# Cross-attention keys and values projected two heads at a time, gates of the linear attention in one piece, skip term by a full matrix of ones

## The chip, the cores and the metric

The kernel runs on one core of a Trainium2 chip. The metric is the device time of one execution in microseconds (us), as the median over repeated runs. Engines are named as in the profile: PE (matrix multiplication, TensorE), DVE (VectorE), ACT (ScalarE), POOL (GpSimd) and SP (the queue that issues nearly all DMAs here). Each engine executes its own instruction stream strictly in order.

## The reference, cut to what matters

A two-layer encoder on 512 tokens of width 1024 (fp32). Each layer adds three mixers (attention, a long convolution called Hyena, gated linear attention), a cross attention into a memory of 256 tokens, and an MLP. The change touches three places: the keys and values of the cross attention, the skip of the long convolution, and the decay gates of the linear attention.

```python
def memory_cross_attention(hn, mn, wq, wk, wv, wo, qn, kn):
    q = rmsnorm((hn @ wq).reshape(B, L, X_HEADS, X_HEAD_DIM), qn)
    k = rmsnorm((mn @ wk).reshape(B, M, X_HEADS, X_HEAD_DIM), kn)   # 4 heads of 256
    v = (mn @ wv).reshape(B, M, X_HEADS, X_HEAD_DIM)
def hyena_filter_spectra(...):
    f = f / (jnp.sum(jnp.abs(f), axis=0, keepdims=True) + EPS)
def long_conv(u, spec, skip):
    return irfft(rfft(u) * spec) + u * skip
def gla_mixer(q, k, v, og, lr, w_lr, b_lr, onorm):
    logit = einsum(lr, w_lr) + b_lr
    g = jax.nn.log_sigmoid(logit) / GLA_NORMALIZER
```

## The kernel before, in words

**Matmuls.** Every fp32 product is three matmuls (`mm3`, L247 to L249): both operands are split into a high and a low part, and high by high, high by low and low by high are added in PSUM. Activations stay in SBUF as such pairs (`xh`/`xl`, for the memory `mnh`/`mnl`). Weights come from HBM in chunks of 128x1024 fp32 (512 KB). For each chunk SP issues a DMA into one of two raw buffers (`wr`), ACT casts it to the high part (`wh`, L231), DVE subtracts to the low part (`wl`, L232), and PE reads both; `wh` and `wl` have three buffers each. `wchunk` (L260) does that for two chunks, which are 256 output columns. A raw buffer is free again when DVE has subtracted, so a late split delays the weights behind it as well.

**Order of the work.** The phases of a layer are generators, and `ORDER0` and `ORDER` say by hand in which order their steps are recorded: `kv` (keys and values of the memory, `cross_kv`), `mx` (`mix_norm`, which makes the normalised input of the layer), `gp` and `gh` (gated linear attention), `at` (attention), `fi` (the filters of the convolution), `ga` (merge gates), `hy`, `me`, `wo`. A scheduler turns this into one stream for each engine. Weight splits are recorded ahead of what stands around them; small matmuls are marked late.

**The pieces touched.** `cross_kv` (L1139) projects the 256 memory tokens head by head, first four heads of v, then four of k: two chunks per head, and 48 matmuls of 256 columns (`mm3` with `wh,mnh`, 2 token tiles x 8 row tiles x 3). ACT evicts v (L1177); for k, ACT squares and sums (L1192), DVE computes a reciprocal root by integer and Newton steps (`rsqrt`, L342, eleven small instructions) and scales (L1197), PE transposes (L1203). Heads of kv stand ahead of `mx` in both lists, so their matmuls are what PE does while DVE and ACT normalise the input: `finish_stat` (L336, a matmul that sums squares over partitions from `hsum`, L328), rsqrt, `tok_bcast` (L358, a matmul that spreads the result), then eight tiles `nrm` (L384) and their split `xh`/`xl` (L242, L243). The first user of the normalised input is the low-rank projection in `gla_proj` (L886).

`filters` (L613) makes the spectra in eight groups (2 layers x 2 orders x 2 halves). The four of layer 0 run inside layer 0's mixers, the four of layer 1 inside layer 0's MLP. At the end of a group (L700 to L720) a matmul with one column of ones sums |f| over partitions into one row of PSUM (L706), two more matmuls make the same sums as columns (L708), DVE adds EPS and multiplies by the skip on that one row of 256 numbers (L712), and a matmul of a row of ones by that row spreads it over 128 partitions into the group's PSUM bank (L718).

`gla_proj` (L868) ends with the gates of four heads. For each: a matmul (L922), Abs on ACT (L925), min on DVE (L927), Exp on ACT (L928), all 128x512; then Ln (L933), a subtraction on POOL (L940), and two cumulative scans on DVE (L941, L943) with POOL copies (L948, L949), then exponentials (L952 to L954) and products on DVE (L959, L960). Exp, Ln and the merge gates' Tanh (L1072) don't share one activation table, so ACT loads a table (ACT_TABLE_LOAD) at a switch.

## Time and profile before

| | before |
|---|---|
| median of 3 runs | 2301.21 us (2300.2 to 2303.95) |
| the profiled execution | 2299.69 us |
| its span, first to last instruction | 2297.8 us |
| PE busy | 2211.1 us, 96% |
| DVE busy | 1535.5 us, 67% |
| ACT busy | 1013.0 us, 44% |
| POOL busy | 418.1 us, 18% |
| mean granted clock of PE | 0.985 |

The profiled execution is 1.5 us below the median. A busy share is a mean over 2.3 ms: stretches in which PE does not pause stand beside short ones in which DVE is busy throughout and PE waits for it. The idle time of an engine is listed with the instruction that ended it.

### The profile page before, as it was taken

Reading aid. Unit: us, or ns where it says so; the run is one execution under the profiler, and the core shown is the slowest. Engines: PE = TensorE matmul, PEld = TensorE weight load, DVE = VectorE, ACT = ScalarE, POOL = GpSimd, SP = SyncE. Lnnn points to the kernel's source line nnn. Section 1 sums busy time; section 2 is a strip of 40 time slices with the busy share of each in tenths; the row PEclk is TensorE's granted clock in tenths of the full one; section 3 lists DMA queues with packets and bytes.
Section 4 is the critical chain, followed back from the end, with each engine's and each line's share of the span. In section 5 each row is a group of like instructions: output and inputs, shape, how many; then the busy total and the mean of one; then the engine's idle time right before and its main releaser. Section 6 shows DMA issues by size and latency. Waiting matters only on the chain.

```text
span 2297.8 us, 29857 instructions
## 1 busy us (share of the span) xinstructions
PE 2211.1 (96%) x11432; PEld 1857.2 (81%) x11432; DVE 1535.5 (67%) x2491; ACT 1013.0 (44%) x1635; POOL 418.1 (18%) x353
## 2 busy tenths in 40 slices
PE   6989999998899999999999989999989999999999
PEld 6877888887678878888887978888867788888887
DVE  7799856869665755766476786667886566444445
ACT  5667744323344544443336577443323444433231
POOL 1141101224220101111051130012253101000004
PEclk9999999999999999999999999999999999999999
DMA  6423123123143133332244321242222422323222
GB/s 224 146 97 106 65 74 123 56 93 101 60 149 113 63 122 103 122 122 101 92 143 143 105 79 41 74 128 65 83 101 74 141 89 74 101 92 101 94 94 97
DMA packets 78966, 232.58 MB, mean 101 GB/s; under 512 B 9054, under 2 KB 10086, under 8 KB 78824
## 3 DMA queue, kind: packets, MB, share of 16 engines
q1 hardware_dynamic: 75656, 224.91, 29.7%
q0 software_dynamic: 3168, 5.77, 0.9%
q8 instruction: 90, 1.47, 0.3%
q14 instruction: 52, 0.43, 0.1%
HBM read 213.87 MB, written 16.78 MB: 100 GB/s over the span
## 4 chain that ended last, share of the span: by engine, by line
PE 78%; DVE 13%; ACT 3%; DMA 2%; issue 2%; POOL 1%; SPq 0%; DVEq 0%; ACTq 0%; POOLq 0%
PE ps L249 24%; PE ps L247 24%; PE ps L248 24%; DVE wl L232 3%; PE ps L533 1%; ACT wh L231 1%; DVE ts L796 1%; PE ps L520 1%; PE ps L542 1%; PE ps L544 1%; DMA wr<-in_x_wv_dram 1%; PE ps L521 1%; DMA F<-F 1%; DVE u L797 1%; DVE ts L587 1%
## 5 line engine op out<-in xcount | busy, mean ns | idle before, releaser
L232 DVE TENSOR_TENSOR wl<-wr,wh 128x1024 fp32r<-128x1024 f32 x340 | 432.7, 1275 | 257.6 <-ACT wh L231 253.1
L231 ACT CAST wh<-wr 128x1024 fp32r<-128x1024 f32 x344 | 357.9, 1042 | 554.1 <-PE ps L248 459.8
L249 PE MATMUL ps<-xh,wl 128*128 128x512 f32 x1344 | 532.8, 397 | 17.2 <-DVE wl L232 17.2
L247 PE MATMUL ps<-xh,wh 128*128 128x512 f32 x1344 | 534.3, 398 | 2.3 <-ACT wh L231 2.0
L248 PE MATMUL ps<-xl,wh 128*128 128x512 f32 x1344 | 532.3, 396 | 0.0
L249 PEld LDWEIGHTS ps<-xh,wl 128*128 128x128 f32 x1344 | 255.4, 190 | 72.6 <-DVE wl L232 20.9
L247 PEld LDWEIGHTS ps<-xh,wh 128*128 128x128 f32 x1344 | 255.6, 190 | 55.7 <-ACT wh L231 3.3
L248 PEld LDWEIGHTS ps<-xl,wh 128*128 128x128 f32 x1344 | 255.6, 190 | 50.4
L249 PE MATMUL ps<-hdh,wl 128*128 128x512 f32 x512 | 199.9, 390 | 0.0
L247 PE MATMUL ps<-hdh,wh 128*128 128x512 f32 x512 | 199.7, 390 | 0.0
L248 PE MATMUL ps<-hdl,wh 128*128 128x512 f32 x512 | 199.2, 389 | 0.0
L1344 DVE TENSOR_TENSOR macc<-ps,macc 128x512 f32<-128x512 f32 x96 | 66.1, 689 | 86.0 <-PE ps L249 86.0
L249 PEld LDWEIGHTS ps<-hdh,wl 128*128 128x128 f32 x512 | 96.1, 188 | 22.1 <-issue 2.3
L248 PEld LDWEIGHTS ps<-hdl,wh 128*128 128x128 f32 x512 | 96.1, 188 | 19.9
L247 PEld LDWEIGHTS ps<-hdh,wh 128*128 128x128 f32 x512 | 96.1, 188 | 19.9 <-issue 0.3
L1346 POOL TENSOR_TENSOR macc<-macc,rb 128x512 f32<-128x512 f32 x16 | 23.6, 1472 | 398.4 <-DVE macc L1344 398.4
L248 PE MATMUL ps<-wl,xh 128*128 128x256 f32 x320 | 91.5, 286 | 0.8 <-DVE wl L232 0.8
L247 PE MATMUL ps<-wh,xh 128*128 128x256 f32 x320 | 91.4, 286 | 0.1
L249 PE MATMUL ps<-wh,xl 128*128 128x256 f32 x320 | 91.3, 285 | 0.0
L248 PE MATMUL ps<-wl,mnh 128*128 128x256 f32 x256 | 77.0, 301 | 13.9 <-DVE wl L232 13.8
L1328 DVE TENSOR_TENSOR rl<-rl 128x512 f32<-128x512 f32 x64 | 44.7, 699 | 65.9 <-ACT rl L1327 65.9
L247 PE MATMUL ps<-wh,mnh 128*128 128x256 f32 x256 | 76.2, 298 | 7.8 <-ACT wh L231 7.8
(404 smaller groups left out, 4570.8 us busy)
## 6 DMA issues: line engine op xcount, KB each, us to landing
wr<-in_mlp_w_dram SPq DMA_DIRECT2D x128, 512.0 KB, 3.5
wr<-in_w_in_dram SPq DMA_DIRECT2D x108, 512.0 KB, 3.6
wr<-in_x_wv_dram SPq DMA_DIRECT2D x16, 512.0 KB, 3.6
wr<-in_x_wk_dram SPq DMA_DIRECT2D x16, 512.0 KB, 4.0
F<-ff SPq DMA_DIRECT2D x32, 256.0 KB, 2.3
F<-F SPq DMA_DIRECT2D x32, 256.0 KB, 5.2
wr<-in_w_out_dram SPq DMA_DIRECT2D x16, 512.0 KB
wr<-in_x_wq_dram SPq DMA_DIRECT2D x16, 512.0 KB, 3.6
```

The costliest lines, as they stand in the source:

```text
L231: r = self.nc.scalar.copy(hi, src)
L232: (lo_eng or self.nc.vector).tensor_tensor(lo, src, hi, op=ALU.subtract)
L247: mm(out, lh, rh, start=start, stop=False, skip_group_check=True)
L248: mm(out, lh, rl, start=False, stop=False, skip_group_check=True)
L249: mm(out, ll, rh, start=False, stop=stop, skip_group_check=True)
L520: nc.tensor.matmul(s, QH[:, tk], K2, start=True, stop=False)
L521: nc.tensor.matmul(s, QL[:, tk], K2, start=False, stop=True)
L533: nc.tensor.transpose(pt[:, k, i * P:(i + 1) * P], Pn[i][:, (2 * kp + k) * P:(2 * kp + k + 1) * P], self.ident)
L542: nc.tensor.matmul(ov, vv, TH[:, k], start=(kt == 0), stop=False, skip_group_check=True)
L1328: nc.vector.tensor_tensor(r, r, r, op=ALU.mult)
L1344: nc.vector.tensor_tensor(acc[m], ps, acc[m], op=ALU.add)
L1346: nc.gpsimd.tensor_tensor(acc[m], acc[m], rb, op=ALU.mult)
```

## The change

Four edits, in the order of the title, and one in the buffers.

1. `cross_kv` projects two heads at once. The host lays `x_wk` and `x_wv` out so that one chunk of 512 KB holds 256 rows by 512 columns. `proj_mem` reads four chunks per pair of heads and issues 48 matmuls of 512 columns into two PSUM banks. Squares, roots and scales follow for two heads together (one rsqrt of four columns where there were two of two). `kv` has five steps where it had nine, and stands in the lists anew: all four heads of v are recorded before `mx`, no head of k.
2. The chunks of `x_wv` go through three raw buffers of their own (`wraw`), issued after the last weight DMA recorded; those of `x_wk` stay in the ring `wr`.
3. The skip is multiplied before the sum over partitions: `hy_skip` comes as 128x256 (128 KB, the row repeated by the host), DVE forms (acc + EPS/128) x skip, ACT and DVE split it, and two matmuls of 256 columns with a 128x128 matrix of ones add it into the group's bank. L706 and L718 go.
4. The gates of four heads lie in one tile `ab` of 128x4x512: four Abs, then one Exp and one Ln of 128x2048.

```diff
-kv kv kv lx kv kv kv mx fi gp gp kv gp fi at at at gp at fi at at at gp ga0 at gp fi kv at kv ga0 at
+kv kv lx kv mx fi gp gp kv gp fi at at at gp at fi at at at gp ga0 at gp fi kv at ga0 at at ga0 at
...
-kv kv kv kv kv kv mx gp gp gp kv at at at at ga0 kv gp at at at ga0 at at gp at ga0 at at at at gp
-at at ga0 at gp gp gp at gh gh gh kv gh gh ga2 gh gh dft hy0 ga2 gh at gh at ga2 gh hy0 gh hy0 hy0
+kv kv kv mx gp gp gp kv at at at at ga0 gp at at at ga0 at at gp at ga0 at at at at gp at at ga0 at
+gp gp gp at gh gh gh kv gh gh ga2 gh gh dft hy0 ga2 gh at gh at ga2 gh hy0 gh hy0 hy0 me0 hy1 gh hy0
...
+    def proj_mem(self, W, hp, X, own):
+        ps = [self.ps("mm") for _ in range(2)]
+        for g in range(4):
+            raw = self.t("wraw", (P, 1024), F32, "wraw") if own else self.wbuf("wr")
+            with self.after(self.last_w) if self.last_w is not None else nullcontext():
+                self.last_w = self.nc.sync.dma_start(raw, W[hp, g])
...
+            with self.tc.high_priority(offset=SPLIT_AHEAD):
+                self.split(raw, hi, lo)
+            for mt in range(2):
+                tk = slice(mt * P, (mt + 1) * P)
+                for k in range(2):
+                    kt = 2 * g + k
+                    self.mm3(ps[mt], X[kt][0][..., tk], X[kt][1][..., tk], hi[:, k], lo[:, k], kt == 0, kt == 7)
+        return ps
...
+                skip = self.skip
+                self.load(skip, I["hy_skip"][l, o, c])
...
+                sa = self.t("F", (P, 2, 256), F32, "skip")[:, 0]
+                nc.vector.scalar_tensor_tensor(sa, acc, EPS / P, skip, op0=ALU.add, op1=ALU.mult)
+                sb = self.t("F", (P, 2, 256), F32R, "skip2")
+                self.split(sa, sb[:, 0], sb[:, 1])
+                with self.late("fr"):
+                    for x in range(2):
+                        nc.tensor.matmul(T4[0][:, 0], self.ones_r, sb[:, x], start=False, stop=(x == 1),
+                                         skip_group_check=True)
...
-                    nc.tensor.matmul(ps[0:1, 0:256], self.ones[:, 0:1], acc, start=True, stop=True)
...
-                row = self.rowbuf
-                self.load(row, I["hy_skip"][l, o, c])
-                nc.vector.scalar_tensor_tensor(row, ps[0:1, 0:256], EPS, row, op0=ALU.add, op1=ALU.mult)
...
-                    nc.tensor.matmul(T4[0][:, 0], self.ones[0:1, :], row, start=False, stop=True,
...
+        xs = self.t("ab4", (P, 4, L), F32, "ab")
         for h in range(4):
...
-            nc.scalar.activation(c, ps, AF.Abs, bias=b)
+            nc.scalar.activation(xs[:, h], ps, AF.Abs, bias=b)
...
-            nc.scalar.activation(c, c, AF.Exp, scale=-1.0)
...
-        for c in xs:
-            nc.scalar.activation(c, c, AF.Ln, bias=self.ones[:, 0:1])
+        nc.scalar.activation(xs, xs, AF.Exp, scale=-1.0)
+        yield
+        nc.scalar.activation(xs, xs, AF.Ln, bias=self.ones[:, 0:1])
...
-        for h in range(4):
-            w = self.wchunk(I["x_wk"][l], h)
...
+        for hp in range(2):
+            ps = self.proj_mem(I["x_wk"][l], hp, X, False)
```

**PE, start of layer 1.** Before, the sums for the normalised input (L336, `hsum`) stand behind 120 matmuls of the values (`wh`/`wl` with `mnh`/`mnl`):

```order
L248 MATMUL ps_10430<-wl_74,mnh_10281 128x256
L249 MATMUL ps_10430<-wh_70,mnl_10282 128x256
L336 MATMUL ps_10625<-consts,hsum_10107 128x1
L247 MATMUL ps_10430<-wh_72,mnh_10248 128x256
L336 MATMUL ps_10625<-consts,hsum_10107 128x1 x3
```

Now the same sums (L360 of the changed kernel) stand behind 15:

```order
L251 MATMUL ps_10116<-wh_73,mnh_10069 128x512
L252 MATMUL ps_10116<-wl_74,mnh_10069 128x512
L253 MATMUL ps_10116<-wh_73,mnl_10070 128x512
L360 MATMUL ps_10264<-ones,hsum_9917 128x1 x4
L251 MATMUL ps_10116<-wh_73,mnh_10069 128x512
```

The broadcast (L358 before, L382 now) follows 18 matmuls later before and 15 later now, and the first user of the normalised input (L886, now L913) stands behind 240 matmuls of 256 columns before (four heads of v, one of k) and behind 96 of 512 columns now (four heads of v).

**DVE, gates of layer 1.** Before, two weight splits (`wl`) stand behind the first scan (L941) of the fourth head:

```order
L943 SCALAR_TENSOR_TENSOR ab_11598<-reset_12221,mn_11600 64x512
L941 SCALAR_TENSOR_TENSOR ab_11605<-reset_12221,mn_11607 64x512
L950 TENSOR_TENSOR ab_11598<-ab_11598,small 128x512
L943 SCALAR_TENSOR_TENSOR ab_11605<-reset_12221,mn_11607 64x512
L941 SCALAR_TENSOR_TENSOR ab_11612<-reset_12221,mn_11614 64x512
L232 TENSOR_TENSOR wl_74<-wr_69,wh_72 128x1024
L232 TENSOR_TENSOR wl_75<-wr_68,wh_70 128x1024
L959 SCALAR_TENSOR_TENSOR qk_1677_10774<-qk_1677_10774,mn_11593 128x512
```

Now two of them stand behind the first scan (L966) of the first head:

```order
L954 TENSOR_SCALAR mn_11186<-ps_11183,consts 128x512
L954 TENSOR_SCALAR mn_11191<-ps_11188,consts 128x512
L966 SCALAR_TENSOR_TENSOR ab_11172<-reset_11795,mn_11176 64x512
L236 TENSOR_TENSOR wl_76<-wr_70,wh_71 128x1024
L236 TENSOR_TENSOR wl_74<-wr_69,wh_72 128x1024
L968 SCALAR_TENSOR_TENSOR ab_11172<-reset_11795,mn_11176 64x512
L966 SCALAR_TENSOR_TENSOR ab_11172<-reset_11795,mn_11181 64x512
```

The next `wl` comes eleven instructions after the last row shown, behind four more scans.

**ACT, gates of layer 1.** Before, between the last two heads' Abs (L925), Exp (L928) and Ln (L933) stand three table loads, and a fourth before L952:

```order
L925 ACTIVATE ab_11612<-ps_11610,consts 128x512
L933 ACT_TABLE_LOAD
L933 ACTIVATE ab_11605<-ab_11605,consts 128x512
L928 ACT_TABLE_LOAD
L928 ACTIVATE ab_11612<-ab_11612 128x512
L1072 ACTIVATE gt_11785<-ps_11760 128x512
L933 ACT_TABLE_LOAD
L933 ACTIVATE ab_11612<-ab_11612,consts 128x512
L231 CAST wh_72<-wr_69 128x1024
L952 ACT_TABLE_LOAD
```

Now one Exp (L956) and one Ln (L958) of 128x2048, with a merge gate's Tanh (L1097, `gt`) between them and two weight casts (L235) behind:

```order
L952 ACTIVATE ab_11172<-ps_11188,consts 128x512
L956 ACTIVATE ab_11172<-ab_11172 128x2048
L1097 ACTIVATE gt_11362<-ps_11337 128x512
L958 ACT_TABLE_LOAD
L958 ACTIVATE ab_11172<-ab_11172,ones 128x2048
L235 CAST wh_71<-wr_70 128x1024
L235 CAST wh_72<-wr_69 128x1024
L1097 ACT_TABLE_LOAD
```

In the whole program ACT has 17 table loads before and 9 now, and PE 11114 rows before and 10732 now.

## Rows read from the trace of the kernel before

**Rows 1.** The page: busy time of the engines; chain that ended last.

```profile
PE 2211.1 (96%) x11432; PEld 1857.2 (81%) x11432; DVE 1535.5 (67%) x2491; ACT 1013.0 (44%) x1635; POOL 418.1 (18%) x353
...
PE 78%; DVE 13%; ACT 3%; DMA 2%; issue 2%; POOL 1%; SPq 0%; DVEq 0%; ACTq 0%; POOLq 0%
```

**Rows 2.** Stretches: length, busy (count) PE, PEld, DVE, ACT, POOL; clock, DMA, GB/s.

```profile
40.00:60.00 20.00, 18.64 (x111) 15.85 (x112) 15.50 (x30) 9.48 (x18) 0.82 (x2) 0.85 0.63 190
...
140.00:160.00 20.00, 16.69 (x65) 12.94 (x66) 19.44 (x35) 16.04 (x22) 9.13 (x13) 0.74 0.26 80
...
660.00:1060.00 400.00, 397.78 (x1883) 327.00 (x1882) 253.77 (x422) 184.89 (x290) 57.06 (x48) 1.00 0.32 105
...
1320.00:1350.00 30.00, 24.75 (x101) 19.89 (x101) 26.83 (x41) 20.13 (x35) 18.27 (x21) 0.89 0.24 79
```

**Rows 3.** PE's waits, whole span: us in total, times, longest us.

```profile
PE ps L249 <- DVE wl L232: 31.4, 16, 5.2
PE ps L248 <- DVE wl L232: 14.6, 9, 5.9
```

**Rows 4.** Timeline of PE, layer 1's first values: start us, us, instruction.

```profile
1195.66 0.28 PE L248 MATMUL ps<-wl,mnh 128*128 128x256 f32 x1
...
1205.02 0.28 PE L248 MATMUL ps<-wl,mnh 128*128 128x256 f32 x1
```

**Rows 5.** Timeline of PE, end of a filter group inside the MLP.

```profile
906.65 0.39 PE L247 MATMUL ps<-hdh,wh 128*128 128x512 f32 x1
...
911.64 0.39 PE L248 MATMUL ps<-hdl,wh 128*128 128x512 f32 x1
...
911.96 0.59 PE L706 MATMUL ps<-acc,consts 128*1 128x256 f32 x2
...
912.48 0.50 PE L249 MATMUL ps<-hdh,wl 128*128 128x512 f32 x1
...
913.50 0.39 PE L248 MATMUL ps<-hdl,wh 128*128 128x512 f32 x1
...
913.82 0.69 PE L718 MATMUL ps<-consts 1*128 1x256 f32 x2
...
914.44 0.50 PE L249 MATMUL ps<-hdh,wl 128*128 128x512 f32 x1
```

**Rows 6.** DVE on consts: ns min/median/max, first and last start, forms.

```profile
L409 DVE TENSOR_TENSOR rtab<-consts,gb x8: 408/419/580, 76.7 to 1253.5; 128x256 f32<-128x256 f32 x8
...
L712 DVE SCALAR_TENSOR_TENSOR consts<-ps,consts x8: 402/411/413, 123.4 to 1062.7; 1x256 f32<-1x256 f32 x8
```

**Rows 7.** Timeline, start of layer 0; brackets: idle before, its releaser.

```profile
40.29 0.58 PE L248 MATMUL ps<-wl,mnh 128*128 128x256 f32 x1 [5.92 <-DVE wl L232]
...
56.98 0.39 PE L886 MATMUL ps<-xh,wh 128*64 128x512 f32 x1
...
47.71 1.05 ACT L231 CAST wh<-wr 128x1024 fp32r<-128x1024 f32 x1 [6.57 <-DMA wr<-in_x_wk_dram]
```

**Rows 8.** Timeline of DVE and PE, start of layer 1.

```profile
1198.48 0.68 DVE L328 TENSOR_TENSOR hsum<-hsum,hsq 128x512 f32<-128x512 f32 x1
...
1231.49 0.75 DVE L243 SCALAR_TENSOR_TENSOR xl<-nrm,consts,xh 128x512 fp32r<-128x512 f32 x1 [0.34 <-ACT xh L242]
...
1209.94 0.28 PE L336 MATMUL ps<-consts,hsum 128*128 128x1 f32 x2
...
1232.80 0.39 PE L886 MATMUL ps<-xh,wh 128*64 128x512 f32 x1
```

**Rows 9.** Timeline of PE and ACT, gates of layer 1.

```profile
1338.87 0.80 PE L249 MATMUL ps<-xh,wl 128*128 128x512 f32 x1 [5.25 <-DVE wl L232]
...
1322.28 0.67 ACT L925 ACTIVATE ab<-ps,consts 128x512 f32<-128x512 f32 x1
...
1322.96 1.28 ACT L933 ACT_TABLE_LOAD   x1
...
1324.26 0.72 ACT L933 ACTIVATE ab<-ab,consts 128x512 f32<-128x512 f32 x1
```

More of the change, by code (lines that the diff above doesn't have):

```diff
@@ L108, in laid_out @@
     o["w_glr"] = chunks(w[:, :, 3840:3872], 32)
-    for n in ("w_br_attn", "w_br_hyena", "w_br_gla", "w_out", "x_wq", "x_wk", "x_wv", "x_wo", "mlp_w1",
-              "mlp_w2"):
+    for n in ("w_br_attn", "w_br_hyena", "w_br_gla", "w_out", "x_wq", "x_wo", "mlp_w1", "mlp_w2"):
         o[n] = chunks(a[n])
+    for n in ("x_wk", "x_wv"):
+        d, k, m = a[n].shape
+        o[n] = f(a[n].reshape(d, k // 256, 2, P, m // 512, 512).transpose(0, 4, 1, 3, 2, 5)).reshape(
+            d, m // 512, k // 256, P, 1024)
     col = lambda x: x.reshape(depth, -1, P).transpose(0, 2, 1)
@@ L271, in wchunk @@
         return parts
+    def proj_mem(self, W, hp, X, own):
[4 more added lines that the diff above has]
+                self.last_w = self.nc.sync.dma_start(raw, W[hp, g])
+            raw = raw.rearrange("p (k n) -> p k n", k=2)
+            hi = self.wbuf("wh").rearrange("p (k n) -> p k n", k=2)
+            lo = self.wbuf("wl").rearrange("p (k n) -> p k n", k=2)
+            with self.tc.high_priority(offset=SPLIT_AHEAD):
[6 more added lines that the diff above has]
+        return ps
     def proj_cm(self, ps, w, cols, X):
@@ L289, in setup @@
         nc, cp = self.nc, self.cp
-        C = cp.tile([P, 1408], F32, name="consts")
-        self.rowbuf = C[0:1, 1152:1408]
+        C = cp.tile([P, 1280], F32, name="consts")
+        self.skip = C[:, 1024:1280]
+        self.ones_r = cp.tile([P, P], F32R, name="ones")
         self.small = cp.tile([P, 2 * SMALL], F32, name="small")
@@ L715, in filters @@
                 nc.vector.reciprocal(rn[:, 2 * c:2 * c + 2], nt)
-                with self.late("fr"):
-                    nc.tensor.matmul(T4[0][:, 0], self.ones[0:1, :], row, start=False, stop=True,
-                                     skip_group_check=True)
                 even = [self.tile_sum("f8", T4[0], held, op) for op in (ALU.add, ALU.subtract)]
@@ L1169, in cross_kv @@
         yield
-        for h in range(4):
-            w = self.wchunk(I["x_wv"][l], h)
-            ps = self.ps("mm", (P, 2, 256))
-            for mt in range(2):
-                self.proj_tm(ps[:, mt], w, slice(0, 256), X, slice(mt * P, (mt + 1) * P))
-            xv = self.t("xv", (P, 2, 256), F32, "xv")
-            for mt in range(2):
-                nc.scalar.activation(xv[:, mt], ps[:, mt], AF.Copy, scale=rm[:, mt:mt + 1])
-            nc.sync.dma_start(self.kvd[4 + h].rearrange("p (a b) -> p a b", a=2), xv)
+        for hp in range(2):
+            ps = self.proj_mem(I["x_wv"][l], hp, X, True)
+            for j in range(2):
+                xv = self.t("xv", (P, 2, 256), F32, "xv")
+                for mt in range(2):
+                    nc.scalar.activation(xv[:, mt], ps[mt][:, 256 * j:256 * j + 256], AF.Copy, scale=rm[:, mt:mt + 1])
+                nc.sync.dma_start(self.kvd[4 + 2 * hp + j].rearrange("p (a b) -> p a b", a=2), xv)
             yield
@@ new lines, in cross_kv @@
+        for hp in range(2):
+            ps = self.proj_mem(I["x_wk"][l], hp, X, False)
+            kks = []
+            ss = self.tiny(4, "kss")
+            for j in range(2):
+                kk = self.t("st", (P, 2, 256), F32, "xk")
+                for mt in range(2):
+                    nc.scalar.activation(kk[:, mt], ps[mt][:, 256 * j:256 * j + 256], AF.Square,
+                                         accum_out=ss[:, 2 * j + mt:2 * j + mt + 1])
+                kks.append(kk)
+            for j in range(2):
+                s2 = ss[:, 2 * j:2 * j + 2]
+                nc.vector.scalar_tensor_tensor(s2, s2, 1.0 / 256, me, op0=ALU.mult, op1=ALU.add)
+            rk = self.tiny(4, "krs")
+            self.rsqrt(rk, ss)
+            for j in range(2):
+                kk = kks[j]
+                for mt in range(2):
+                    nc.vector.scalar_tensor_tensor(kk[:, mt], ps[mt][:, 256 * j:256 * j + 256],
+                                                   rk[:, 2 * j + mt:2 * j + mt + 1], G, op0=ALU.mult, op1=ALU.mult)
+            for j in range(2):
+                kk = kks[j]
+                pt = self.ps("b", (P, 2, 256))
+                for dt in range(2):
+                    for mt in range(2):
+                        with self.late("kt"):
+                            nc.tensor.transpose(pt[:, dt, mt * P:(mt + 1) * P],
+                                                kk[:, mt, dt * P:(dt + 1) * P], self.ident)
+                xk = self.t("xk", (P, 2, 256), F32, "xk")
+                nc.scalar.copy(xk, pt)
+                nc.sync.dma_start(self.kvd[2 * hp + j].rearrange("p (a b) -> p a b", a=2), xk)
```

46 lines of the change are left out of this document (11 added, 35 removed).

## The prediction

> **What bounds the kernel now.** I read the page first, then the table of stretches, PE's waits, and last the timelines of the places that the change touches. PE is busy 96% of the span and leads the chain that ended last with 78%; DVE has 13% of that chain [rows 1]. So a matmul removed counts in full wherever PE does not pause, and elsewhere only if DVE keeps up. The stretches show which is which [rows 2]: from 660 to 1060 us PE is busy 397.78 of 400, while from 140 to 160 DVE is busy 19.44 of 20, PE 16.69, and the granted clock is 0.74; from 1320 to 1350 DVE has 26.83 of 30 and PE 24.75 at 0.89. Nearly all that PE waits for is the low half of a weight, split on DVE: 31.4 and 14.6 us [rows 3]. The changed instructions lie in both kinds of stretch.
>
> About 0.2% (4.6 us) is what a measurement of this kernel can tell from no change.
>
> **The stream of keys and values.** There are 2 layers x 8 heads x 48 = 768 matmuls of 256 columns, and there will be 384 of 512. The printed durations (0.28 and 0.39) overlap, so I take starts. In the first values of layer 1 there are 78 steps from 1195.66 to 1205.02: 0.120 us each [rows 4]. Of 512 columns there are 22 steps from 906.65 to 911.64: 0.2268 us each [rows 5]. So 768 x 0.120 = 92.2 us become 384 x 0.2268 = 87.1: **-5.1 us**, on PE's own path. The Trainium skill ("TensorE: Matmul & The Clock Gate", section "Back-to-back issue gap") gives N/2.4 + 2.5 ns as the gap of a warm matmul, 109.2 and 215.8 ns; by that estimate the wider form would save only 1.0 us and the sum below would be 4.1 us smaller. Both rows lie above those gaps, and the measured spacings decide.
>
> The evictions read the same elements. Per layer two rsqrt chains of eleven small DVE instructions go, off PE's path: nothing. A pair fills two banks, so the second pair of values may wait for the first one's eviction; six matmuls of the other bank (1.4 us) stand between, so nothing, and at most as much again per layer if ACT is late.
>
> **The skip, eight groups.** In the MLP the matmul L706 stretches the step between its neighbours from 0.227 to 0.84 us (911.64 to 912.48), and L718 stretches one to 0.94 (913.50 to 914.44) [rows 5]: 0.61 + 0.71 = 1.32 us go. Two matmuls of 256 columns come, 2 x 0.120 = 0.24: -1.08 a group. Four groups lie in the MLP, where PE does not pause: **-4.3**. The other four lie in layer 0's mixers, where DVE is about as full as PE. There PE would gain 4.3 again, while DVE gets a product and a subtraction of 128x256 (0.42 each by the nearest row) for the row product of 0.41 [rows 6], +0.43 a group, 1.7 in all. Between -4.3 and +1.7 I take the middle, **-1.3**. ACT's extra cast and the 128 KB instead of 1 KB (8 loads, issued early in a group) lie beside that work: nothing. If their load came late, the product would wait, and behind it on DVE the weight splits: that is part of the upper end.
>
> **Start of layer 0.** PE waits 5.92 us for a split at 40.29, queued on DVE behind the normalisation; then an ACT cast waits 6.57 us for a chunk of `x_wk` until 47.71, with casts of the normalised input queued behind it; L886, the first user of that input, starts at 56.98 with one head of k done [rows 7]. In the new order no chunk of `x_wk` stands there, and the values have raw buffers of their own, so both delays can shrink; but half a k pair (24 x 0.2268 = 5.4 us) must now be made up after the first user. If all of both went, -7; if the input came no earlier, +5.4. I take **-2.5**: most of the cast's wait, little of the split's, as the subtractions still share DVE with the normalisation.
>
> **Start of layer 1.** `hsum` is ready at 1199.2 (1198.48 + 0.68), but the sums over it, L336, wait in PE's order until 1209.94, behind 120 matmuls; the last piece of the normalised input starts on DVE at 1231.49 and its user L886 at 1232.80 [rows 8]. Behind 15 matmuls (3.4 us) they start at about 1199, some 10 us earlier, so the input may be complete near 1222 and not 1232. PE has then had only 96 x 0.2268 = 21.8 us of values from 1195.7 and will be idle from about 1217.5 to 1222. First user at 1222 instead of 1232.8, less 5.4 for the key head that is now behind it: -5, and of that the stream's 1.6 is counted already. I take **-3**. The ends are +5.4 (input no earlier) and -8 (the split stalls inside the normalisation go too).
>
> **The gates.** ACT has 17 table loads in its order before and 9 after. A load takes 1.28 us; the Abs before one ends at 1322.95, the load runs from 1322.96, the Ln starts at 1324.26 [rows 9]: nothing but the load itself shows. Eight fewer are 10.3 us of ACT, which is PE's bound nowhere, but in layer 1 two or three of them lie in the chain to the scans. The Trainium skill ("ScalarE: Activation LUTs", section "What ACT_TABLE_LOAD costs") adds a drain of about 1.38 us to each switch; eight switches would be 21.3 us by that estimate, and the 0.02 us behind the load here speaks against it. In layer 1 PE stalls 5.25 us at 1338.87 for a split behind the scans [rows 9], and the clock of 0.89 over 30 us adds 3.3. In the new order a split stands behind one scan only, but that scan waits for the Ln of all four heads, and the split after it has four more scans ahead. All of it gone is -8.5; a stall of the same kind twice as long is +6; I take **-3**. In layer 0 the idle 3.3 us (20 - 16.69) and 0.26 x 20 = 5.2 of clock [rows 2] are at stake, with DVE full throughout; between -8 and +5 I take **-2**.
>
> **Sum:** -5.1 - 4.3 - 1.3 - 2.5 - 3 - 3 - 2 = -21.2 us, against the profiled execution of 2299.69: 2278.5. The median stands 1.5 us above that execution: **2280**.
>
> **Rivals.**
> - *Only the matmuls count.* DVE stays full around the normalisation and the gates, and every stall that goes comes back one split later. For it: DVE's 19.44 of 20 and PE's waits, of which nearly all end with a split. Against: in layer 1 the sums wait for PE's order and for nothing else. -5.1 - 4.3 - 1.3 = -10.7: 2290.5.
> - *The gates in one piece are the longer wait.* The first scan now waits for four heads; splits queued behind scans come later still, +6 in layer 1 and +5 in layer 0. With the starts as forecast: -10.7 - 5.5 + 11 = -5.2: 2296.
> - *The other side: the normalised input loses its cover.* One head of k, the work that PE had before the first user, is moved behind it. If the input is ready no earlier than 56.98 and 1232.8, both heads (5.4 each) come on top, and PE restarts at the lower clock after the idle time: from 40 to 60 us, after a stall of 5.92, the clock is 0.85, 3.0 us lost [rows 2, 7]. -10.7 + 10.8 + 6 and nothing from the gates: +6, 2307. It decides where the input is complete later than about 1227 in layer 1, the point at which the gain equals the head moved. Against it: the 10 us that L336 waits in order alone.
>
> **How the numbers follow.** Forecast 0.55, only the matmuls 0.24, longer gates 0.12, cover lost 0.09. Faster by over 0.2% (below 2296.6) takes the first two and half of the third: 0.84; within 0.2%: 0.08; slower: 0.08. The range reaches down to 2264, where the two starts and the gates of both layers give three quarters of their lower ends (0.75 x -31.5 = -23.6) and the matmuls their best (-5.1 - 4.3 - 4.3 = -13.7), and up to 2299, which takes in both rivals below the time of before; what it leaves out above is the lost cover.
>
> **What would show it.** The k and v matmuls 0.227 us apart, 384 of them; no one-column matmul in the filter groups; nine table loads; in layer 1 the sums over `hsum` at about 1199 less what was gained earlier, and the first user of the input some 23 us later, after a pause of about 5; no PE wait above 3 us in either layer's gates. I am wrong if PE still waits 5 us for a split at these places, or if the pause before the first user is over 10 us.

## The result, and the profile after

| | before | changed |
|---|---|---|
| median | 2300.7 us (2300.11 to 2303.95, 4 runs) | 2284.59 us (2280.7 to 2287.47, 4 runs) |
| ratio | | 0.9928 (95% interval 0.9916 to 0.9941) |
| the profiled execution's span | 2297.8 us | 2283.4 us |

The kernel became 0.72% faster, about 16.6 us; forecast were 21.2, and 2284.59 lies in the range. The two profiled spans differ by 14.4 us, and the account below is made of them.

The page of the changed kernel, busy time and chain, against [rows 1]:

```profile
PE 2197.6 (96%) x11032; PEld 1831.6 (80%) x11032; DVE 1533.5 (67%) x2455; ACT 1001.0 (44%) x1623; POOL 422.6 (19%) x353
...
PE 78%; DVE 14%; issue 3%; ACT 2%; DMA 2%; POOL 1%; SPq 0%; DVEq 0%; POOLq 0%; ACTq 0%
```

PE lost 400 instructions and 13.5 us of busy time, and its share stayed at 96%. The waits of PE (total, times, longest, in us), against [rows 3]:

```profile
PE ps L253 <- DVE wl L236: 32.3, 18, 4.6
PE ps L251 <- ACT wh L235: 13.0, 7, 7.5
PE ps L252 <- DVE wl L236: 8.6, 4, 3.0
```

The subtractions of weights still end most of its idle time: 32.3 and 8.6 us where they were 31.4 and 14.6. So the stalls were moved more than removed. Stretches (columns as in [rows 2]):

```profile
140.00:160.00 20.00, 16.11 (x62) 12.17 (x60) 19.86 (x18) 8.91 (x15) 13.20 (x12) 0.91 0.27 83
660.00:1060.00 400.00, 398.24 (x1905) 330.63 (x1904) 262.87 (x439) 185.07 (x294) 55.20 (x49) 1.00 0.35 110
```

The MLP stretch is as tight as before. The stretch from 140 to 160 us still has PE at 16.11 with DVE at 19.86. ACT has nine table loads, as forecast.

To see where the time went I compare the start of the same PE instruction in both traces at points where the scheduling around it is alike. A difference that grows is a gain between two points.

| point on PE (line before / after) | before, us | after, us | difference |
|---|---|---|---|
| first filter matmul of layer 0 (L669 / L695) | 101.29 | 92.72 | -8.6 |
| first gate matmul, layer 0 (L922 / L950) | 126.81 | 117.35 | -9.5 |
| first transpose of the linear attention heads, layer 0, all keys done (L1005 / L1030) | 314.99 | 308.35 | -6.6 |
| sums over `hsum` after layer 0's mixers (L336 / L360) | 691.95 | 687.29 | -4.7 |
| fifth filter group, in the MLP (L669 / L695) | 878.66 | 872.11 | -6.5 |
| last column sums in the MLP (L708 / L742) | 1062.62 | 1051.67 | -10.9 |
| memory sums, start of layer 1 (L1160 / L1185) | 1194.65 | 1182.91 | -11.7 |
| first gate matmul, layer 1 (L922 / L950) | 1280.24 | 1262.36 | -17.9 |
| sixth group of convolution transposes, layer 1, all keys done (L768 / L795) | 1559.06 | 1544.65 | -14.4 |

Both starts gained more than forecast, the MLP's four filter groups what was forecast, and the two stretches of gates lost time instead of gaining it. Each column is one execution. Between kernels whose code in a stretch is the same, a stretch differs by up to some 4 us (the experiments show where), so a difference of that size in one row proves nothing by itself.

**The stream.** Timeline of PE, last values of layer 1: 26 steps from 1204.02 to 1209.92, 0.2269 us each, as taken from [rows 5].

```profile
1204.02 0.39 PE L251 MATMUL ps<-wh,mnh 128*128 128x512 f32 x1
...
1209.92 0.39 PE L253 MATMUL ps<-wh,mnl 128*128 128x512 f32 x1
```

**The skip.** Timeline of PE at the end of a filter group in the MLP, against [rows 5]:

```profile
905.43 0.39 PE L251 MATMUL ps<-hdh,wh 128*128 128x512 f32 x1
905.66 0.28 PE L736 MATMUL ps<-skip,ones 128*128 128x256 f32 x1
905.77 0.28 PE L742 MATMUL ps<-ones,acc 128*128 128x1 f32 x2
905.91 0.48 PE L252 MATMUL ps<-hdl,wh 128*128 128x512 f32 x1
...
906.49 0.48 PE L253 MATMUL ps<-hdh,wl 128*128 128x512 f32 x1
906.80 0.39 PE L251 MATMUL ps<-hdh,wh 128*128 128x512 f32 x1
```

Three steps of 512 columns, 905.43 to 906.80, take 1.37 us instead of 3 x 0.227 = 0.68, with all the small matmuls of the group among them: 0.69 over. Before, the four steps from 911.64 to 914.44 took 2.80 instead of 0.91: 1.89 over. What goes is 1.20, near the 1.08 taken.

**The starts.** Timeline of PE in layer 0, a pause for a split and the first user of the normalised input, against [rows 7]:

```profile
26.10 0.79 PE L252 MATMUL ps<-wl,mnh 128*128 128x512 f32 x1 [1.67 <-DVE wl L236]
...
41.97 0.42 PE L913 MATMUL ps<-xh,wh 128*64 128x512 f32 x1 [1.93 <-DVE wh L236]
```

L913 starts at 41.97 instead of 56.98. The pause of 1.67 is no remainder of the 5.92 at 40.29 in [rows 7]: before the change it stood there too, at 27.23.

```profile
27.23 0.38 PE L248 MATMUL ps<-wl,mnh 128*128 128x256 f32 x1 [1.57 <-DVE wl L232]
```

Behind it PE waits for no weight of the values any more; 1.93 us go to the small weight of L913 itself, which DVE splits between pieces of the input. In layer 1, against [rows 8]:

```profile
1187.46 1.05 PE L360 MATMUL ps<-ones,hsum 128*128 128x1 f32 x8
...
1201.39 0.50 PE L252 MATMUL ps<-wl,mnh 128*128 128x512 f32 x1 [3.02 <-DVE wl L236]
...
1210.82 0.39 PE L913 MATMUL ps<-xh,wh 128*64 128x512 f32 x1
```

The sums stand 4.6 us behind the memory sums and the first user comes 27.9 us after them (before: 38.2). The pause is 3.02 us and is ended by a split, not by the input. The first user follows the last matmul of the values without a pause.

**The gates.** The forecast named as a sign that no wait of PE in either layer's gates is above 3 us. In layer 0 the longest is 2.97. In layer 1 the wait for a split has shrunk from 5.25 us [rows 9] to 1.82, but 5 us behind it a wait of 3.82 has come for a cast of q on ACT, so the sign was missed. Its chain, on POOL, DVE, ACT and PE:

```profile
1321.70 3.57 POOL L982 TENSOR_TENSOR small<-small 128x4 f32<-128x4 f32 x1
...
1326.67 0.69 DVE L975 TENSOR_TENSOR ab<-ab,small 128x512 f32<-128x512 f32 x1 [1.47 <-POOL small L974]
...
1327.39 0.63 ACT L977 ACTIVATE mn<-ab 128x512 f32<-128x512 f32 x1 [3.31 <-DVE ab L975]
...
1325.26 0.50 PE L253 MATMUL ps<-xh,wl 128*128 128x512 f32 x1 [1.82 <-DVE wl L236]
...
1330.27 1.22 PE L544 MATMUL ps<-k,qh 128*128 128x512 f32 x2 [3.82 <-ACT qh L532]
```

The cast of q (ACT, 1329.07) stands behind an exponential of the gates (L977), which waits for a product on DVE, which waits for a copy on POOL; POOL had been held up by a product of 128x4 that took 3.57 us, where one in layer 0 takes 0.20 (at 161.20).

### The profile page after: what moved, and what is told of

Read it like the earlier page. It is cut to its first block, busy times and chain, and to the rows that moved or that the text cites. A ratio compares the mean times of both kernels' runs of the same rounds, so it can differ in the third digit from the quotient of the medians.

```text
span 2283.4 us, 28957 instructions
## 1 busy us (share of the span) xinstructions
PE 2197.6 (96%) x11032; PEld 1831.6 (80%) x11032; DVE 1533.5 (67%) x2455; ACT 1001.0 (44%) x1623; POOL 422.6 (19%) x353
## 4 chain that ended last, share of the span: by engine, by line
PE 78%; DVE 14%; issue 3%; ACT 2%; DMA 2%; POOL 1%; SPq 0%; DVEq 0%; POOLq 0%; ACTq 0%
PE ps L251 24%; PE ps L253 24%; PE ps L252 24%; DVE wl L236 3%; PE ps L557 1%; DVE ts L823 1%; ACT wh L235 1%; PE ps L566 1%; DMA F<-F 1%; PE ps L568 1%; DVE u L824 1%; PE ps L544 1%; DVE ts L611 1%; PE ps L545 0%; DMA wr<-in_w_in_dram 0%
## 5 line engine op out<-in xcount | busy, mean ns | idle before, releaser
L236 DVE TENSOR_TENSOR wl<-wr,wh 128x1024 fp32r<-128x1024 f32 x324 | 415.1, 1284 | 244.0 <-ACT wh L235 239.7
L235 ACT CAST wh<-wr 128x1024 fp32r<-128x1024 f32 (+1 forms) x328 | 341.0, 1042 | 507.1 <-PE ps L252 424.2
L352 POOL TENSOR_TENSOR hsum<-hsum,hsq 128x512 f32<-128x512 f32 x30 | 43.6, 1454 | 168.3 <-ACT hsq L350 168.3
L1357 ACT ACTIVATE rl<-ps 128x512 f32<-128x512 f32 x64 | 37.9, 592 | 77.9 <-PE ps L253 77.9
```

The source lines that it names most:

```text
L235: r = self.nc.scalar.copy(hi, src)
L236: (lo_eng or self.nc.vector).tensor_tensor(lo, src, hi, op=ALU.subtract)
L352: eng.tensor_tensor(self.hsum, self.hsum, sq, op=ALU.add)
L1357: nc.scalar.activation(r, ps, AF.Relu)
```

## The experiments

Twelve kernels ran, each compared with the kernel before; ratios are to that one, and 0.001 is 2.3 us. "Lost time" in the expectations is the length of a stretch less its matmuls at the spacing they have where PE runs freely.

**1. Gates head by head.** The changed kernel, with Exp and Ln as before.

```diff
-        xs = self.t("ab4", (P, 4, L), F32, "ab")
...
+            c = self.t("f8", name="ab")
+            nc.scalar.activation(c, ps, AF.Abs, bias=b)
...
+            nc.scalar.activation(c, c, AF.Exp, scale=-1.0)
...
+        for c in xs:
+            nc.scalar.activation(c, c, AF.Ln, bias=self.ones[:, 0:1])
```

> The changed kernel with the gates as before it: Exp and Ln head by head, 128x512 each, in four tiles of their own. Theory A (the gates in one piece make the first scan wait for all four heads, and that is what gave back about 6 us of PE time between the first and the last of layer 0's gates and heads, and 1 to 4 us in layer 1): 5 to 9 us faster than the changed kernel, and PE's lost time in layer 0's stretch falls from 31 to about 25 us. Theory B (the loss there comes from the k pair or the skip on a full DVE, the table loads saved are worth something): the same or up to 4 us slower.

Measured: 2282.42 us, 0.9915 (0.9902 to 0.9929). That is 0.0013 below the change, inside the intervals. In layer 0 the stretch from the gates to the heads is as long as with the gates in one piece (190.9 and 191.1 us), so Theory A falls there. In layer 1 the difference to the kernel before moves from -16.2 at the first gate matmul to -19.0 at the sixth transposes, where the change moved from -17.9 to -14.4. But there the profiles differ among themselves by 3 us: that stretch is 278.8 us before and 282.3 in the change, but 279.1 and 279.2 in experiments 3 and 4, which have the same gates. With the gates head by head it is 276.0 here, 276.6 and 276.1 in experiments 5 and 11, and 279.5 in experiment 6, whose profiled execution was the longest of its five. The waits go with the form of the gates: in one piece 1.8 us for a split and 2.9 to 3.8 for the cast of q (the change, experiments 3, 4 and 8), head by head one wait of 4.6 to 4.8 for a split (experiments 1, 5, 6 and 11). So in layer 0 the form of the gates is not what costs; in layer 1, by these traces, the one piece may cost some 3 us, which the two medians can't tell from nothing.

**2. Gates in halves.**

```diff
-        nc.scalar.activation(xs, xs, AF.Exp, scale=-1.0)
+            if h % 2:
+                nc.scalar.activation(xs[:, h - 1:h + 1], xs[:, h - 1:h + 1], AF.Exp, scale=-1.0)
...
+        for h in (0, 2):
+            nc.scalar.activation(xs[:, h:h + 2], xs[:, h:h + 2], AF.Ln, bias=self.ones[:, 0:1])
```

> The changed kernel with Exp and Ln over two heads at a time (128x1024). Theory A: between the two, 2 to 5 us faster than the changed kernel. Theory B: within 2 us of it.

Measured: 2284.03 us, 0.9928 (0.9916 to 0.9941), the same as the change. Theory B.

**3. The skip as a row.** The changed kernel with the old skip.

```diff
-                nc.vector.scalar_tensor_tensor(sa, acc, EPS / P, skip, op0=ALU.add, op1=ALU.mult)
...
-                        nc.tensor.matmul(T4[0][:, 0], self.ones_r, sb[:, x], start=False, stop=(x == 1),
...
+                    nc.tensor.matmul(ps[0:1, 0:256], self.ones[:, 0:1], acc, start=True, stop=True)
...
+                nc.vector.scalar_tensor_tensor(row, ps[0:1, 0:256], EPS, row, op0=ALU.add, op1=ALU.mult)
...
+                    nc.tensor.matmul(T4[0][:, 0], self.ones[0:1, :], row, start=False, stop=True,
```

> The changed kernel with the skip as before it (one-column matmul, product on one row, matmul by a row of ones, load of 1 KB). Theory A (the two matmuls cost PE 1.08 us a group wherever they stand): 8 to 9 us slower than the changed kernel, about 4.3 of it in the MLP of layer 0. Theory B (in layer 0's mixers DVE pays instead, so half of it is worth nothing): 4 to 6 us slower, all of it in the MLP.

Measured: 2295.65 us, 0.9975 (0.9966 to 0.9984), so 10.8 us slower than the change. The filter groups in the MLP carry what was forecast: from the fifth filter matmul to the last column sums PE takes 184.0 us instead of 179.6. Layer 0's stretch of gates and heads takes 191.7 instead of 191.1: there the matmuls are worth little, as Theory B has it. What neither theory has is 3 us at each of two short pauses elsewhere. The next pieces show one: a wait before a filter matmul inside the MLP, and the stretches of 10 us around and behind it. In this kernel:

```profile
839.73 1.90 PE L649 MATMUL ps<-sa,consts 64*64 64x512 f32 x2 [2.04 <-ACT sa L634]
```

```profile
833.00:843.00 10.00, 7.96 (x26) 4.95 (x25) 6.31 (x9) 6.13 (x10) 3.85 (x5) 0.84 0.20 64
843.00:853.00 10.00, 10.00 (x38) 8.09 (x37) 6.77 (x11) 3.98 (x6) 0.00 (x0) 0.82 0.34 107
```

In the changed kernel, the same place:

```profile
834.69 1.07 PE L649 MATMUL ps<-sa,consts 64*64 64x512 f32 x2 [1.46 <-ACT sa L634]
```

```profile
833.00:843.00 10.00, 8.54 (x36) 6.24 (x35) 7.72 (x12) 5.93 (x8) 0.00 (x0) 1.00 0.25 59
```

Behind the pause of 1.46 us the granted clock stayed at 1.00; behind the one of 2.04 it was 0.84 and 0.82, and 3.4 us were lost. The length of the pause is not what decides it: in the traces of experiments 1 and 9 the same pause is 2.04 us long and the clock stays at 1.00 (shown in the last section). So of the 10.8 the trace shows 4.4 in the MLP's groups, 1 to 2 in the mixers, and lower clock behind pauses. As the clock falls at this pause with the new skip too (experiments 2, 4 and 10), I don't count those microseconds as the skip's, though that isn't shown for the median.

**4. The values in the common ring.**

```diff
-            ps = self.proj_mem(I["x_wv"][l], hp, X, True)
+            ps = self.proj_mem(I["x_wv"][l], hp, X, False)
```

> The changed kernel with the chunks of x_wv in the common ring of two raw buffers. Theory A (the new order alone brings the normalised input forward): within 2 us of the changed kernel, first user of the normalised input at about the same time in both layers. Theory B (the three buffers are what makes the starts shorter): 5 to 10 us slower, with the first user 3 to 5 us later in both layers.

Measured: 2287.77 us, 0.994 (0.9926 to 0.9954), some 3 us slower, between the two theories, and the intervals overlap. Timeline of PE in layer 0:

```profile
38.77 0.50 PE L252 MATMUL ps<-wl,mnh 128*128 128x512 f32 x1 [2.81 <-DVE wl L236]
...
47.67 0.42 PE L913 MATMUL ps<-xh,wh 128*64 128x512 f32 x1
```

The first user of the input comes 5.7 us later than in the change, after a pause of 2.81 that the change doesn't have. The first filter matmul comes at 100.29 (101.29 before), where the nine kernels in the new order with the three buffers (the change among them) have it between 92.7 and 95.7. In layer 1 the user stands 28.0 us behind the memory sums, as in the change (27.9). So by this trace the buffers make the start of layer 0 (Theory B) and the order makes that of layer 1 (Theory A). The medians differ by less than these 5 to 7 us; where the rest goes I don't know.

**5. The keys later.** Gates head by head, and the second pair of keys of layer 0 behind the third step of the heads.

```diff
-kv kv lx kv mx fi gp gp kv gp fi at at at gp at fi at at at gp ga0 at gp fi kv at ga0 at at ga0 at
-at at fi at at at gp ga0 gp at gp gh gh gh gh gh ga2 gh gh dft hy0 ga2 gh at gh at ga2 gh hy0 gh hy0
+kv kv lx kv mx fi gp gp kv gp fi at at at gp at fi at at at gp ga0 at gp fi at ga0 at at ga0 at
+at at fi at at at gp ga0 gp at gp gh gh gh kv gh gh ga2 gh gh dft hy0 ga2 gh at gh at ga2 gh hy0 gh hy0
```

> The changed kernel with the gates head by head and, in the first layer's list, the second pair of keys moved from before the attention blocks to after the third step of the linear attention heads, where DVE has room. Theory A (the stretch from layer 0's gates to its heads, 191 us long for 160 us of PE work, is as long as DVE's 179 us of work and its waits; PE work removed there is worth nothing, DVE work moved out is worth its length): the pair's 7 to 9 us of DVE leave the stretch, PE's lost time there falls from 31 to 23 to 27 us, and the kernel is 4 to 8 us faster than with the gates head by head alone. Theory B (PE's order in that stretch, not DVE, makes the pauses): PE loses its filler, the stretch is shorter by the pair's 10.9 us of matmuls or less, and the total is the same or slower.

Measured: 2289.98 us, 0.9951 (0.9939 to 0.9964), 8 us slower than without the move. Stretches from the gates to the heads, and from there to the convolution, here:

```profile
118.30:300.40 182.10, 166.04 (x984) 141.26 (x982) 157.29 (x267) 130.91 (x248) 53.69 (x54) 0.96 0.26 85
300.40:383.00 82.60, 80.06 (x424) 67.20 (x423) 48.19 (x103) 32.48 (x56) 9.69 (x11) 0.94 0.31 94
```

and with the gates head by head alone:

```profile
117.50:308.40 190.90, 176.46 (x1032) 150.09 (x1030) 162.30 (x288) 134.62 (x262) 52.02 (x53) 0.96 0.29 92
308.40:372.70 64.30, 64.30 (x374) 54.93 (x374) 39.35 (x81) 25.80 (x41) 8.95 (x11) 1.00 0.31 95
```

The first stretch is shorter by 8.8 us where 10.9 of matmuls left it, the second longer by 18.3. DVE's 5 us fewer in the first didn't free PE. Theory B: by these traces the stretch is not bound by how much DVE has to do in all.

**6. Keys and values alone.** The old skip and the old gates: the diffs of experiments 1 and 3 together.

> The changed kernel with the old skip and the old gates, so only the keys and values (two heads wide, new order, three raw buffers). Theory A (the start of layer 0 gains 6 us and the DVE-full stretch takes them back; the stream's 5.1 us and layer 1's start remain): 7 to 11 us faster than before, with PE's lost time in layer 0's stretch at 29 to 31 us as in the full change. Theory B (the loss in that stretch comes with the skip's extra DVE work): 10 to 14 us faster, lost time there 25 to 27 us.

Measured: 2291.2 us, 0.9964 (0.9951 to 0.9978), 8.3 us faster than before. The profiled execution of this kernel was itself 2301.8 us, so I read its trace for nothing but the stretch of the gates, 193.7 us long. That speaks for Theory A, weakly, as that execution was the longest of five: the loss there comes without the new skip.

**7. The skip alone**, on the kernel before: the diff of experiment 3 turned round, with the load of 128x256 and the matrix of ones.

> The kernel before with the new skip alone. Theory A (1.08 us a group on PE in the MLP, next to nothing in layer 0's DVE-full mixers): 4 to 6 us faster than before. Theory B (1.08 us in all eight groups): 8 to 9 us faster.

Measured: 2299.2 us, 0.9994 (0.9985 to 1.0003), so less than 3.5 us. The groups in the MLP take 179.6 us, the 4.4 again. In this trace two losses take it back: the first filter matmul comes 4.5 us later (105.76), and layer 0's stretch grows from 188.2 to 191.7. The gain in the MLP is sure. That the skip makes the losses is not: with other edits the stretch in the old order is 186.2 (experiment 8) or 192.4 (experiment 12). The whole is less than Theory A forecast.

**8. The gates in one piece alone**, on the kernel before: the diff of experiment 1 turned round.

> The kernel before with the gates in one piece alone. Theory A (nothing in layer 0, where DVE sets the pace; a longer wait of the first scan in layer 1, 2 to 4 us): 1 to 4 us slower than before. Theory B (the table loads saved count): 2 to 6 us faster.

Measured: 2298.64 us, 0.9991 (0.9983 to 1.0): between no change and 4 us faster. Theory A is out; the lower end of Theory B is not.

**9. The subtraction on DVE.** What experiments 1 to 8 had left standing was layer 0's stretch. Its timeline on DVE in the changed kernel:

```profile
139.50 5.79 DVE L498 TENSOR_TENSOR q<-q,small 128x512 f32<-128x512 f32 x4
...
146.34 2.33 DVE L236 TENSOR_TENSOR wl<-wr,wh 128x1024 fp32r<-128x1024 f32 x2
```

and on POOL:

```profile
139.88 4.86 POOL L965 TENSOR_TENSOR mn<-mn,ab 128x512 f32<-128x512 f32 x3 [3.71 <-ACT ab L958]
```

Four products on q (L498) take 5.79 us while POOL subtracts (L965) from 139.88: the first, begun before POOL, 0.69, the other three 1.78 each. The same four took 2.50 us in layer 1, and before the change 2.49 us in layer 0. The splits (`wl`) stand behind them.

```diff
-            nc.gpsimd.tensor_tensor(g, g, c, op=ALU.subtract)
+            nc.vector.tensor_tensor(g, g, c, op=ALU.subtract)
```

> The changed kernel with one engine name changed: the subtraction of the gates (four of 128x512 after the one Ln) on DVE instead of POOL. Theory A (the burst of four POOL subtractions stretches DVE's work beside it: the four products on q there took 1.45 us each in layer 0 against 0.62 in layer 1, and a scan or a split 2.3 instead of 1.2): 2 to 5 us faster than the changed kernel, those products at 0.6 to 0.7 us, and the first scan no later. Theory B (DVE is the full engine; 4 x 0.7 us more work per layer there costs more than the sharing): the same or 1 to 4 us slower.

Measured: **2272.25 us**, 0.9869 (0.9853 to 0.9886), 13.6 us faster than the change and 30 us faster than before. The same place on DVE:

```profile
141.83 2.50 DVE L498 TENSOR_TENSOR q<-q,small 128x512 f32<-128x512 f32 x4
144.24 1.29 DVE L965 TENSOR_TENSOR mn<-mn,ab 128x512 f32<-128x512 f32 x2
145.45 2.36 DVE L236 TENSOR_TENSOR wl<-wr,wh 128x1024 fp32r<-128x1024 f32 x2
```

Four products take 2.50 us again, two subtractions 1.29, and the two splits end 6.0 us after the products start (145.45 + 2.36 - 141.83), where they ended 9.2 us after them (146.34 + 2.33 - 139.50). The stretch:

```profile
119.70:300.60 180.90, 172.49 (x1032) 146.55 (x1030) 159.32 (x292) 131.52 (x254) 42.17 (x50) 0.99 0.29 97
```

against that of the change, 191.1 us long with DVE at 165.06. PE's waits:

```profile
PE ps L253 <- DVE wl L236: 28.8, 17, 4.4
...
PE ps L252 <- DVE wl L236: 5.2, 3, 3.0
```

The wait of 2.97 us in layer 0 is gone; in layer 1 the 1.82 are 0.74 and the 3.82 for the cast of q are 2.38, and the stretch there, from the first gate matmul to the sixth transposes, takes 276.5 us instead of 282.3.

Theory A in direction: DVE did more instructions in less time. But the gain is far above what it forecast, and the products beside POOL, 3.3 us of DVE, can't be all of it.

**10. The same with the gates head by head.**

> Gates head by head, and the subtraction on DVE. Theory A: 2 to 4 us faster than with the gates head by head alone. Theory B: the same or slower, as the POOL subtractions of single heads don't come in a burst.

Measured: 2272.77 us, 0.9878 (0.9863 to 0.9892), 8.5 us faster than experiment 1 and the same as experiment 9. Theory A in direction, again for more than it forecast. So POOL's subtractions cost without the burst too (8.5 and 13.6 are not told apart by the intervals), and with them gone the form of the gates makes no difference.

**11. The second pair of keys in two steps.** Gates head by head; `proj_mem` pauses after two chunks for that pair, and an attention block stands between (in layer 1 the two steps follow one another).

```diff
+            if hp == 1 and g == 1 and not own:
+                yield
...
-kv kv lx kv mx fi gp gp kv gp fi at at at gp at fi at at at gp ga0 at gp fi kv at ga0 at at ga0 at
+kv kv lx kv mx fi gp gp kv gp fi at at at gp at fi at at at gp ga0 at gp fi kv at kv ga0 at at ga0 at
```

> Gates head by head, and the second pair of keys of layer 0 recorded in two steps of two chunks with an attention block between them, as the two heads stood before the change. Theory A (four chunks in one go, 5 us of splits, are what DVE can't deliver in layer 0's mixers): PE's lost time from the gates to the heads of layer 0 falls from 31 to 25 to 28 us, 3 to 6 us faster than with the gates head by head alone. Theory B (the pauses there belong to the weights of the gates' stretch, not to the pair): within 2 us.

Measured: 2281.36 us, 0.9913 (0.9898 to 0.9928), as in experiment 1 (0.9915). Theory B.

**12. The subtraction on DVE, in the kernel before.**

```diff
-            nc.gpsimd.tensor_tensor(g, g, c, op=ALU.subtract)
+            nc.vector.tensor_tensor(g, g, c, op=ALU.subtract)
```

> The kernel before with the subtraction of the gates on DVE instead of POOL and nothing else. Theory A (sharing with POOL cost as much in the old order; the change neither made it nor moved it): 8 to 13 us faster than before, PE's lost time in layer 0's stretch from 25 to 15 to 20 us. Theory B (the new order brought the subtractions beside the query products and the weight splits, and that is what gave the 6 us back): 0 to 4 us faster, lost time in that stretch about 21 to 25 us, as in the new order with DVE's subtraction.

Measured: 2301.65 us, 1.0 (0.9991 to 1.001). In the total Theory B: in the old order the move gives nothing. Layer 0's stretch (and, second, the filter groups in the MLP), first in the kernel before and then with the subtraction on DVE:

```profile
126.80:315.00 188.20, 177.24 (x1086) 150.71 (x1084) 162.25 (x292) 135.99 (x261) 43.41 (x54) 0.97 0.26 88
...
878.70:1062.60 183.90, 183.90 (x875) 151.15 (x873) 122.82 (x191) 80.14 (x116) 30.80 (x24) 1.00 0.32 107
```

```profile
128.20:320.60 192.40, 181.68 (x1096) 154.33 (x1094) 161.03 (x295) 136.74 (x262) 43.44 (x50) 0.97 0.27 86
```

It became 4.2 us longer, which Theory B did not have either (it expected 21 to 25 us of lost time, 29 are left). Layer 1's stretch became 3.4 us shorter, again first before:

```profile
1280.20:1559.10 278.90, 270.78 (x1666) 237.14 (x1664) 195.90 (x364) 159.99 (x294) 44.39 (x49) 0.98 0.26 82
```

```profile
1284.20:1559.60 275.40, 270.58 (x1665) 237.04 (x1663) 195.76 (x367) 159.74 (x294) 37.03 (x45) 0.99 0.27 83
```

What the move does to the two stretches, in us:

| order and gates | layer 0 | layer 1 |
|---|---|---|
| old order, head by head (experiment 12) | +4.2 | -3.4 |
| new order, in one piece (experiment 9) | -10.1 | -5.8 |
| new order, head by head (experiment 10) | -5.8 | -2.9 |

So the orders differ in layer 0; in layer 1 head by head the move gives about the same in both. It isn't that POOL left DVE alone in the old order. There a scan (1.22 us alone) also took twice as long beside POOL's subtractions:

```profile
134.84 2.56 POOL L940 TENSOR_TENSOR mn<-mn,ab 128x512 f32<-128x512 f32 x2 [0.74 <-ACT ab L933]
...
136.18 2.30 DVE L941 TENSOR_TENSOR_SCAN ab<-reset,mn 64x512 f32<-64x512 f32 x1 [2.39 <-POOL mn L940]
```

Taking every DVE instruction beside one of POOL's eight subtractions, less the time of the same instruction alone, gives 6.4 us before, 7.9 in the changed kernel and 4.7 with its gates head by head; done on DVE the eight take 5.5. DVE's busy time over the whole kernel falls by 7.3 us with the move in the new order with the gates in one piece (1533.5 to 1526.2). With the gates head by head it stays: 1529.1 and 1528.9 in the new order, 1535.5 and 1535.8 in the old. So the load on DVE does not tell the 8.5 us of the one from the nothing of the other. What is left is what waits behind those instructions, or the longer way over POOL; no run here separates the two.

## Why the prediction was right, and where it was off

**The stream, -5.1.** 384 matmuls 0.2269 us apart, as taken. Right.

**The skip.** In the MLP -4.3 was forecast, and the stretch of the four groups is 4.3 to 4.5 us shorter with the new skip in every pair of kernels (183.9 before; here the changed kernel and its layer 0 stretch):

```profile
117.30:308.40 191.10, 175.00 (x1032) 148.42 (x1031) 165.06 (x288) 131.20 (x254) 50.14 (x54) 0.97 0.29 92
...
872.10:1051.70 179.60, 179.60 (x868) 151.08 (x866) 124.73 (x196) 79.26 (x120) 26.43 (x24) 1.00 0.35 112
```

In layer 0's mixers -1.3 was taken, between -4.3 and +1.7. Experiment 3 puts it between -0.6 and -1.9 (with the group that stands ahead of the gates), experiment 7 in the old order at +2.2 (with that group) to +3.5: the term is of the size of the scatter.

**The starts.** -2.5 and -3 were taken, besides the stream's 1.9 (six heads) in each. Measured: -8.6 - (-1.9) = -6.7 by the first filter matmul of layer 0, and -6.1 + 1.9 = -4.2 in layer 1. The signs were right and the first was undersized: I took "most of the cast's wait, little of the split's", and both went; the stall of 5.92 has no counterpart. By the trace of experiment 4 the three buffers did it. The 6.7 is at the upper end, as the other kernels with these buffers have that filter matmul up to 3 us later. In layer 1 the estimate held: first user at 1222 less the 11.7 gained earlier is 1210.3, measured 1210.82; the last piece of the input is ready on DVE at 1209.9. The idle time of about 5 us ahead of it did not come, since a split held the values up for 3.02.

**The gates, -2 and -3.** Wrong: the gain did not come. From the first gate matmul to the point where all keys are done the change lost 2.8 us in layer 0 and 3.5 in layer 1, though the stream's 0.6 for two heads and, in layer 0, the skip are in there; in layer 1 the loss is 0.3 to 0.4 in experiments 3 and 4, which have the same gates, so neither loss is clear of the scatter. The step that failed is "All of it gone is -8.5 ... I take **-3**", and the -2 beside it: it looked at where the splits stand on DVE and at the table loads, and left out the way of the gates over POOL. In layer 1 the stall behind the scans shrank as forecast, from 5.25 to 1.82, but 3.82 came at the next cast of q. The rival "gates in one piece are the longer wait" named the first part of this, and it can be seen where DVE idles for POOL's first subtraction, which itself waited for the Ln of all four heads (POOL, 1304.66):

```profile
1305.99 2.30 DVE L966 TENSOR_TENSOR_SCAN ab<-reset,mn 64x512 f32<-64x512 f32 x1 [7.07 <-POOL mn L965]
1308.21 4.67 DVE L236 TENSOR_TENSOR wl<-wr,wh 128x1024 fp32r<-128x1024 f32 x2
```

In layer 0 experiments 1 and 2 show that the one piece is not what costs: head by head (190.9) and in halves (192.3) the stretch is no shorter than in one piece (191.1). Moving the subtraction to DVE gives 13.6 and 8.5 us (experiments 9 and 10) and gives nothing in the old order (experiment 12). So where POOL's subtractions stand in the new order, they cost, most of all in layer 0; the 5.79 us above show part of it in one place, for the gates in one piece. By what way they cost the rest, and how they cost head by head, where the products on q take 2.5 us, stays open.

**Not forecast.** Between 315 and 692 us the difference shrank from 6.6 to 4.7 us without an edit there, most of it at one wait for a cast of the convolution's input (3.03 us before, 4.43 after). I didn't follow it.

Between the two profiled spans the account is: -21.2 forecast; the starts gave 4.2 + 1.2 = 5.4 more; layer 0's gates and mixers 6.7 less (+2.8 where -2, -1.3 and the stream's -0.6 stood), layer 1's 7.1 less (+3.5 for -3.6); 1.9 were lost between 315 and 692; and the MLP gave 2.6 beyond the skip, 2.1 of it at the pause of experiment 3, where the clock fell before (51.1 us from there to the fifth group) and did not in the change (49.0). That is -13.5 where 14.4 were measured between the spans and 16.6 between the medians. "Only the matmuls count" (2290.5) would have been missed by 6 us. The lost cover did not come: the input was complete in time in both layers.

That the total came within 5 us of the forecast is in part luck. The two stretches of gates, with the mixers' skip, were 13.8 us worse than taken; 5.4 more from the starts and 2.6 in the MLP stood against that. The clock's 2.1 are no work of the change: with the code of before that place takes 48.8 us in experiments 8 and 12.

## What to carry to other kernels

Before a step is moved on a hand-ordered kernel, list what POOL executes beside DVE at its new place, not only what stands in front of it in each queue. The sum of DVE's work does not say what a share moved between the two is worth: head by head that sum stayed (1529.1 and 1528.9 us) and the time fell by 8.5. Price an edit by its stretch: the same exchange of two matmuls was worth 4.4 us where PE runs freely and about 1 in the new order where it waits for splits. And when an order and a work placement change together, try the placement again under the new order: the one-line move that was worth nothing before was worth 13.6 us after.

## What the runs showed that I had not expected

**Sharing between DVE and POOL.** Four DVE products of two SBUF operands, 0.62 us each (2.50 for four), took 5.79 us while POOL subtracted (0.69 for the first, begun before POOL, 1.78 for each of the others), and the weight splits 2.3 us instead of 1.2 in the gates of layer 1 (two in 4.67 us, above). The Trainium skill ("SBUF — State Buffer", section "Who interferes with whom") says that a `tensor_tensor` on DVE with both inputs in SBUF contends with POOL's reads, and that the loser is blocked for the other's whole instruction; the trace agrees, the three products beside POOL having lasted about as long as one POOL subtraction there (1.47 to 1.74 us, 1.3 alone).

**Short pauses and the clock.** In all these kernels PE waits at one place in the MLP for a cast of `sa` on ACT. Behind a pause of 1.46 us (five traces) the clock stayed at 1.00. Behind one of 2.04 it fell in five traces (experiments 2, 3, 4, 6 and 10), to 0.84 and 0.82 over the next two stretches of 10 us in experiment 3, which is 6.8 us at the lower level (1.2 GHz) and cost 3.4 us, more than the pause. In two others, experiments 1 and 9, the clock stayed at 1.00 behind the same pause. Experiment 9:

```profile
828.61 1.07 PE L649 MATMUL ps<-sa,consts 64*64 64x512 f32 x2 [2.04 <-ACT sa L634]
```

```profile
836.00:846.00 10.00, 10.00 (x46) 8.29 (x45) 6.74 (x10) 6.01 (x9) 0.00 (x0) 1.00 0.30 92
```

So the length of the pause alone does not decide it, and kernels that don't touch that place differ by such a step: from there to the fifth filter group the change took 49.0 us (823.08 to 872.11), with the gates in halves it was 52.8. That is the size of the scatter between the stretches above.
